# Loading the 1024-byte-piece weight tiles of a two-layer decoder kernel through two DMA queues

## The chip, the cores and the metric

The kernel runs on one core of one Trainium2 chip. The metric is the device time of one execution in microseconds (us); lower is better. Before the change the median of 3 runs is 270.51 us (270.24 to 270.66).

## The reference, cut to what matters

Two residual layers over 256 tokens of width 1024, all in float32. Each layer normalizes x, multiplies it with one wide input matrix, runs two attention groups on the columns, gates both and multiplies with an output matrix:

```python
for layer in range(DEPTH):                       # DEPTH = 2
    h = rmsnorm(x, norm_gain[layer])
    if layer % 2 == 0:
        proj = h @ w_in_ab[j]                    # 1024 x 4104
        qa, ka, va, ga, qb, kb_, vb_, gb, fb = split_cols(proj, AB_SIZES)
        ...                                      # MoBA attention ya, forgetting attention yb
        y = jnp.concatenate([ya * jax.nn.silu(ga), yb * jax.nn.silu(gb)], axis=-1)
        x = x + y @ w_out_ab[j]                  # 1024 x 1024
    else:
        proj = h @ w_in_cd[j]                    # 1024 x 3328
        qc, kc, vc, gc, qd, kd, vd, gd = split_cols(proj, CD_SIZES)
        ...                                      # differential attention yc, sliding-window attention yd
        y = jnp.concatenate([yc * jax.nn.silu(gc), yd * jax.nn.silu(gd)], axis=-1)
        x = x + y @ w_out_cd[j]
```

## The kernel before

All weights stream from HBM once, in 74 tiles of 512 KB. A tile is a list of parts (column offset, source slice), a number `nk` of 128-row blocks and a width. `wraws` (line 98) loads a tile into a float32 buffer `raw`: each of the 128 partitions receives `nk` rows of the matrix, so the DMA moves 128 x `nk` pieces of (width x 4) bytes. There are four `raw` buffers. `wload` (line 115) then splits the tile for float32-like accuracy: ScalarE (ACT) casts it to `whi` (line 123) and VectorE (DVE) subtracts, giving `wlo` (line 124). Five pairs of `whi`/`wlo` exist. TensorE (PE) multiplies three times per tile and row block (lines 261 to 263, or 430 and 432 for the gates).

Tiles come in three shapes: the first eight have pieces of 4096 bytes (`nk` = 1), most have pieces of 2048 bytes (`nk` = 2, 512 columns), and 22 have pieces of 1024 bytes (`nk` = 4, 256 columns). These 22, counted from 0 in the order of loading, are tiles 16 to 19 (the columns of `kb`, with 4 more columns copied in by GpSimd from `wf`, line 105), 24 to 31 (gates a and b), 52 and 53 (`kd` and `vd`), and 58 to 65 (gates c and d).

Every load is issued by the sync engine (SP) in tile order; SP waits at each for the `raw` buffer to come free, which is when DVE has made the `wlo` of the tile four places earlier. GpSimd (POOL) issues five small DMAs at the start (`params`, line 75, and `bcast`, line 81) and makes the four `wf` copies; after 43 us it has nothing to do.

The order of the work on PE is written out by hand (`tick`, line 149, steps through a list of units; generators such as `qk_heads`, line 342, `quad64`, line 528, and `scores`, line 477, are advanced between them). ACT and DVE run their instructions in the order in which they are issued there, so a cast that waits for its tile holds back what stands behind it. Around tiles 16 to 19 ACT's order is: cast of tile 16, `v`, `qf`, `qhi`, cast of tile 17, `kf` (line 392), first half of `khi` (line 399), cast of tile 18, second half of `khi`, cast of tile 19. On DVE the `wlo` of tile 18 stands ahead of the second half of `klo` (line 400), and `klo` ahead of the `wlo` of tile 19. PE needs `khi` and `klo` for the first attention scores (lines 490 and 494), which stand in its order behind tile 14's products and ahead of tile 15's.

Of the kernel before, what the change touches and what calls it, by code (L numbers as in the profile page):

```python
# [29 lines left out]
def trunk_kernel(  # L30
# [6 lines left out]
    nc = tc.nc  # L37
# [48 lines left out]
    last = {}  # L86
# [11 lines left out]
    def wraws(parts, nk, n, raw=None):  # L98
        if raw is None:
            raw = wraw.tile([128, WF], F32, name="raw")  # L100
        rv = raw[:, 0:nk * n].rearrange("p (k n) -> p k n", k=nk)
        for (c0, src) in parts:
            if isinstance(src, tuple):
                k0, f0 = src
                nc.gpsimd.tensor_copy(rv[:, :, c0:c0 + 4], wf[:, k0:k0 + nk, f0:f0 + 4])
                continue
            m = src.shape[1]
            last["sp"] = nc.sync.dma_start(rv[:, :, c0:c0 + m],
                                           src.rearrange("(k p) n -> p k n", p=128))
        k = len(wt) - KT  # L110
        if 0 <= k < KT:
            nc.sync.dma_start(wf[:, k, :], w_ab[k * 128:(k + 1) * 128, 4096:4104])
        return raw

    def wload(parts, nk, n, raw=None, pieces=1):
        if raw is None:
            raw = wraws(parts, nk, n)
        hi = wsp.tile([128, WF], F32R, name="whi")
        lo = wsp.tile([128, WF], F32R, name="wlo")
        m = nk * n // pieces  # L120
        for i in range(pieces):
            c = slice(i * m, (i + 1) * m)
            last["act"] = nc.scalar.copy(hi[:, c], raw[:, c])  # L123
            last["dve"] = nc.vector.tensor_tensor(out=lo[:, c], in0=raw[:, c], in1=hi[:, c].bitcast(F32),  # L124
                                    op=OP.subtract)
        return (hi[:, 0:nk * n].rearrange("p (k n) -> p k n", k=nk),
                lo[:, 0:nk * n].rearrange("p (k n) -> p k n", k=nk))
# [722 lines left out]
    with tc.manual_schedule():  # L850
        nc.vector.memset(wz, 0.0)
        raws = []
        for n in ("yth", "ytl"):
            r = act.tile([128, 2, 1024], F32, name=n)
            raws += [r[:, 0, :], r[:, 1, :]]
        xload(0)
        wraws(*tiles[0], raws[0])
        xload(1)
        for i in range(1, 4):
            wraws(*tiles[i], raws[i])  # L860
# [115 lines left out]
```

## Time and profile before

| what | value |
|---|---|
| median of 3 runs | 270.51 us (270.24 to 270.66) |
| the profiled execution's own time | 272.91 us |
| span of its profile, first to last instruction | 271.1 us |
| TensorE busy | 263.3 us, 97% of the span |
| mean granted TensorE clock | 0.994 |
| DMA, mean over the span | 153 GB/s |
| weight loads from `w_in_ab`, median issue to landing | 8.5 us |
| weight loads from `w_in_cd`, median issue to landing | 3.9 us |

Times inside the profile count from the first instruction. The own time of the profiled execution holds 1.81 us outside the span. A matmul's end is modelled: one of 512 columns is shown with some 0.39 us, while the next one starts 0.23 us after it, so back-to-back matmuls overlap in the rows and PE's idle time is only what is left between them. The granted clock is the share of full TensorE clock that the chip gave in a stretch.

### The profile page before, as it was taken

What the parts mean: (1) busy time and instruction counts of PE and PEld (TensorE: products, weight loads), DVE (VectorE), ACT (ScalarE), POOL (GpSimd) and SP (SyncE); (2) the same over time, 40 slices, a digit from 0 to 9 for tenths busy, and PEclk for the clock granted to TensorE, in tenths of its full rate; (3) what the DMA queues carried; (4) which work ended last, traced back from release to release, by engine and by line L of the source; (5) the groups of instructions that cost most, each with busy time, mean ns of one, the idle gap of its engine ahead of it and who ended that gap; (6) DMA issues with size and microseconds to landing.
All of it is one profiled execution on the core that took longest, in us unless ns stands there. A gap on an engine that the chain in (4) does not pass through costs nothing.

```text
span 271.1 us, 4378 instructions
## 1 busy us (share of the span) xinstructions
PE 263.3 (97%) x1535; PEld 216.7 (80%) x1535; DVE 213.1 (79%) x501; ACT 183.6 (68%) x411; POOL 6.3 (2%) x14
## 2 busy tenths in 40 slices
PE   7999999979999999999999999999999999999994
PEld 3787788769988688887788888888988789897884
DVE  5887895477997549997946988677898989899722
ACT  3788755676796757899726564457777999999300
POOL 4000040000000000000000000000000000000000
PEclk9999999979999999999999999999999999999999
DMA  6966964770363552814634668655418027207022
GB/s 247 336 196 166 302 182 112 263 221 3 98 182 105 149 167 58 251 27 143 210 104 166 175 183 290 201 160 167 146 34 274 6 77 232 81 8 224 2 77 77
DMA packets 27415, 41.36 MB, mean 153 GB/s; under 512 B 2801, under 2 KB 14466, under 8 KB 27394
## 3 DMA queue, kind: packets, MB, share of 16 engines
q1 hardware_dynamic: 27202, 41.07, 49.2%
q8 instruction: 12, 0.20, 0.3%
q14 instruction: 9, 0.07, 0.1%
q0 software_dynamic: 160, 0.01, 0.0%
q10 hardware_dynamic: 32, 0.01, 0.0%
HBM read 40.03 MB, written 1.05 MB: 152 GB/s over the span
## 4 chain that ended last, share of the span: by engine, by line
PE 74%; DMA 10%; DVE 8%; ACT 4%; issue 2%; SPq 1%; ACTq 0%
PE pj L261 16%; PE pj L263 16%; PE pj L262 16%; DMA raw<-in_w_in_ab_dram 9%; PE pj L430 8%; PE pj L432 4%; DVE wlo L124 3%; PE av L564 3%; PE at L522 3%; PE at L494 2%; PE at L382 2%; DMA wf<-in_w_in_ab_dram 1%; ACT e L505 1%; ACT e L503 1%; ACT whi L123 1%
## 5 line engine op out<-in xcount | busy, mean ns | idle before, releaser
L124 DVE TENSOR_TENSOR wlo<-raw,whi 128x1024 fp32r<-128x1024 f32 (+1 forms) x70 | 85.3, 1222 | 20.6 <-ACT whi L123 18.7
L123 ACT CAST whi<-raw 128x1024 fp32r<-128x1024 f32 (+1 forms) x70 | 72.8, 1048 | 31.0 <-PE pj L262 23.5
L261 PE MATMUL pj<-whi,hh 128*128 128x512 f32 (+2 forms) x192 | 72.8, 379 | 0.8 <-ACT whi L123 0.8
L263 PE MATMUL pj<-wlo,hh 128*128 128x512 f32 (+2 forms) x192 | 70.9, 369 | 0.2 <-DVE wlo L124 0.2
L262 PE MATMUL pj<-whi,hh 128*128 128x512 f32 (+2 forms) x192 | 70.8, 368 | 0.0
L430 PE MATMUL pj<-hh,whi 128*128 128x512 f32 x128 | 46.1, 401 | 0.2 <-DVE g L437 0.2
L261 PEld LDWEIGHTS pj<-whi,hh 128*128 128x128 f32 x192 | 36.5, 190 | 7.7 <-ACT whi L123 0.9
L263 PEld LDWEIGHTS pj<-wlo,hh 128*128 128x128 f32 x192 | 36.4, 189 | 7.5 <-DVE wlo L124 1.2
L262 PEld LDWEIGHTS pj<-whi,hh 128*128 128x128 f32 x192 | 36.4, 190 | 5.8 <-DVE hh L225 0.2
L432 PE MATMUL pj<-hh,wlo 128*128 128x256 f32 x128 | 35.8, 280 | 0.0
L430 PEld LDWEIGHTS pj<-hh,whi 128*128 128x128 f32 x128 | 24.1, 188 | 6.0 <-DVE g L437 0.4
L261 PE MATMUL pj<-whi,yth 128*128 128x512 f32 (+1 forms) x68 | 26.3, 387 | 0.0
L263 PE MATMUL pj<-wlo,yth 128*128 128x512 f32 (+1 forms) x68 | 25.9, 381 | 0.0
L262 PE MATMUL pj<-whi,ytl 128*128 128x512 f32 (+1 forms) x68 | 25.8, 380 | 0.0
L432 PEld LDWEIGHTS pj<-hh,wlo 128*128 128x128 f32 x128 | 24.2, 189 | 0.0
L503 ACT ACTIVATE e<-e,mn 128x128 f32<-128x128 f32 x32 | 12.5, 391 | 7.8 <-DVE mn L499 7.8
L505 ACT ACTIVATE e<-e,mn 128x256 f32<-128x256 f32 x32 | 15.9, 496 | 0.2 <-DVE mn L501 0.2
L261 PEld LDWEIGHTS pj<-whi,yth 128*128 128x128 f32 x68 | 12.8, 188 | 2.8 <-issue 0.3
L263 PEld LDWEIGHTS pj<-wlo,yth 128*128 128x128 f32 x68 | 12.8, 188 | 2.6
L262 PEld LDWEIGHTS pj<-whi,ytl 128*128 128x128 f32 x68 | 12.8, 188 | 2.5
L346 ACT ACTIVATE sq<-pj 128x512 f32<-128x512 f32 (+2 forms) x18 | 8.9, 509 | 4.3 <-PE pj L263 3.8
L347 DVE TENSOR_REDUCE qk_m<-sq 128x8 f32<-128x512 f32 (+2 forms) x18 | 10.1, 577 | 1.8 <-ACT sq L346 1.7
(159 smaller groups left out, 373.5 us busy)
## 6 DMA issues: line engine op xcount, KB each, us to landing
raw<-in_w_in_ab_dram SPq DMA_DIRECT2D x28, 512.0 KB, 8.5
raw<-in_w_in_cd_dram SPq DMA_DIRECT2D x26, 512.0 KB, 3.9
raw<-in_w_out_ab_dram SPq DMA_DIRECT2D x8, 512.0 KB, 5.3
raw<-in_w_out_cd_dram SPq DMA_DIRECT2D x8, 512.0 KB, 3.8
xs<-in_x_dram SPq DMA_DIRECT2D x2, 512.0 KB, 5.9
yth<-in_w_in_ab_dram SPq DMA_DIRECT2D x2, 512.0 KB, 6.8
ytl<-in_w_in_ab_dram SPq DMA_DIRECT2D x2, 512.0 KB, 7.7
out_dram<-xs SPq DMA_DIRECT2D x3, 256.0 KB, 2.0
```

Source lines behind the costliest of these rows:

```text
L123: last["act"] = nc.scalar.copy(hi[:, c], raw[:, c])
L124: last["dve"] = nc.vector.tensor_tensor(out=lo[:, c], in0=raw[:, c], in1=hi[:, c].bitcast(F32), op=OP.subtract)
L261: nc.tensor.matmul(ps, ah, bh, start=first, stop=False)
L262: nc.tensor.matmul(ps, al, bh, start=False, stop=False)
L263: nc.tensor.matmul(ps, ah, bl, start=False, stop=last)
L346: nc.scalar.activation(sq[:, 0:nh * HD], ps[t][:, 0:nh * HD], AF.Square)
L347: nc.vector.tensor_reduce(m[:, t, :], sq[:, 0:nh * HD].rearrange("p (h d) -> p h d", d=HD), axis=AX.X, op=OP.add)
L430: nc.tensor.matmul(pg, wh[:, i, w], hh[:, k].rearrange("p u t -> p (u t)"), start=k == 0, stop=False)
L432: nc.tensor.matmul(pg[:, 0:256], wl[:, i, w], hh[:, k, 0, :], start=False, stop=k == KT - 1)
L503: nc.scalar.activation(e[:, 0:128], e[:, 0:128], AF.Exp, bias=mn[:, 0:1], scale=-1.0, accum_out=sm[:, 0:1])
L505: nc.scalar.activation(e[:, 128:384], e[:, 128:384], AF.Exp, bias=mn[:, 1:2], scale=-1.0, accum_out=sm[:, 1:2])
L522: nc.tensor.transpose(pt[:, i * 128:(i + 1) * 128], blocks[j + i], ident)
```

## The change

In `wraws`, a part that is 256 columns wide is no longer loaded by one DMA of SP. GpSimd issues a DMA for the second half of its row blocks (two of four), and SP one for the first half. All other loads stay as they were. The consumer of a tile now waits for both.

```diff
             m = src.shape[1]
-            last["sp"] = nc.sync.dma_start(rv[:, :, c0:c0 + m],
-                                           src.rearrange("(k p) n -> p k n", p=128))
+            sv = src.rearrange("(k p) n -> p k n", p=128)
+            if m == 256:
+
+                nc.gpsimd.dma_start(rv[:, nk // 2:nk, c0:c0 + m], sv[:, nk // 2:nk, :])
+                last["sp"] = nc.sync.dma_start(rv[:, 0:nk // 2, c0:c0 + m], sv[:, 0:nk // 2, :])
+                continue
+            last["sp"] = nc.sync.dma_start(rv[:, :, c0:c0 + m], sv)
```

The order of instructions on PE, DVE and ACT is the same before and after. On GpSimd, before the change, the four copies of tiles 16 to 19 (`raw_601`, `raw_659`, `raw_687`, `raw_727`) stand right behind the small DMAs of the start:

```order
L75 DMA prow_88<-in_moba_k_gain_dram 1x2x64
L75 DMA prow_88<-in_fox_q_gain_dram 1x2x64
L75 DMA prow_88<-in_fox_k_gain_dram 1x2x64
L81 DMA bfor_303<-in_b_forget_dram 128x8
L105 COPY raw_601<-wf_89 128x4x4
L105 COPY raw_659<-wf_89 128x4x4
L105 COPY raw_687<-wf_89 128x4x4
L105 COPY raw_727<-wf_89 128x4x4
```

After it, each copy stands behind the DMA of its tile's second half, and 18 more such DMAs follow (tiles 24 to 31, 52, 53 and 58 to 65):

```order
L75 DMA prow_88<-in_fox_k_gain_dram 1x2x64
L81 DMA bfor_303<-in_b_forget_dram 128x8
L111 DMA raw_601<-in_w_in_ab_dram 128x2x256
L105 COPY raw_601<-wf_89 128x4x4
L111 DMA raw_660<-in_w_in_ab_dram 128x2x256
L105 COPY raw_660<-wf_89 128x4x4
L111 DMA raw_689<-in_w_in_ab_dram 128x2x256
L105 COPY raw_689<-wf_89 128x4x4
L111 DMA raw_730<-in_w_in_ab_dram 128x2x256
L105 COPY raw_730<-wf_89 128x4x4
L111 DMA raw_1045<-in_w_in_ab_dram 128x2x256
```

The copies have moved behind one DMA issue each; nothing else of GpSimd's has moved. On ACT, around tiles 16 to 18, the casts wait after the change for a DMA of each kind (DMAHW is SP's, DMASW is GpSimd's; the line numbers are five higher than before):

```order
L414 ACTIVATE v_530<-pj_427,n_r_334 128x512 [waits PE_49]
L128 CAST whi_605<-raw_601 128x1040 [waits DMASW5_49,DVE_49,DMAHW3_49,PE_49,Pool_49]
L414 ACTIVATE v_530<-pj_428,n_r_334 128x512 [waits PE_49]
L397 ACTIVATE qf_107<-at_533,pcol_90 128x512 [waits PE_49]
L404 ACTIVATE qhi_108<-at_539,pcol_90 128x512 [waits PE_49]
L128 CAST whi_664<-raw_660 128x1040 [waits DMASW6_49,DVE_49,DMAHW4_49,PE_49,Pool_49]
L397 ACTIVATE kf_110<-at_567,pcol_90 128x512 [waits PE_49]
L404 ACTIVATE khi_111<-at_567,pcol_90 128x4x128
L128 CAST whi_693<-raw_689 128x1040 [waits DVE_49,DMASW7_49,PE_49,DMAHW5_49,Activation_49,Pool_49]
```

Before the change the same casts stood at the same places and waited for SP's DMA alone; what moved is only which DMAs they wait for.

## Rows read from the trace of the kernel before

**Rows 1.** The page: span, and the first row of the engines' busy time.
```profile
span 271.1 us, 4378 instructions
...
PE 263.3 (97%) x1535; PEld 216.7 (80%) x1535; DVE 213.1 (79%) x501; ACT 183.6 (68%) x411; POOL 6.3 (2%) x14
```

**Rows 2.** The chain that ended last, 40 to 62 us: start us, us, what.
```profile
40.24 12.79 DMA raw<-in_w_in_ab_dram
...
53.13 1.06 ACT whi L123
...
55.38 0.76 DVE klo L400
...
56.18 0.39 PE at L494 x2
...
57.43 0.72 PE pj L261
...
60.48 0.23 PE pj L262
...
61.64 0.12 PE pj L261
```

**Rows 3.** Timeline of PE, the first scores (53 us) and the second (71 us).
```profile
53.63 0.49 PE L490 MATMUL at<-kf,qf 64*128 64x128 f32 x4
...
57.36 0.79 PE L261 MATMUL pj<-whi,hh 128*128 128x512 f32 x1
...
71.51 0.49 PE L490 MATMUL at<-kf,qf 64*128 64x128 f32 x4
...
72.07 0.28 PE L494 MATMUL at<-klo,qhi 64*128 64x256 f32 x2
...
72.87 0.39 PE L261 MATMUL pj<-whi,hh 128*128 128x260 f32 x1
```

**Rows 4.** Windows: stretch us, PE, PEld, DVE, ACT, POOL busy (x), PEclk, DMA share, GB/s.
```profile
41.00:46.50 5.50, 5.50 (x30) 4.59 (x29) 2.92 (x5) 2.13 (x3) 0.20 (x1) 1.00 0.38 107
49.00:51.50 2.50, 2.50 (x15) 2.04 (x14) 0.88 (x2) 1.62 (x3) 0.00 (x0) 1.00 0.88 306
...
57.40:60.20 2.80, 2.80 (x9) 2.22 (x8) 2.09 (x16) 2.69 (x13) 0.00 (x0) 0.52 0.85 267
...
184.25:185.50 1.25, 1.25 (x7) 1.03 (x6) 1.25 (x2) 0.60 (x1) 0.00 (x0) 1.00 0.99 345
```

**Rows 5.** Timeline of ACT: the cast of tile 17, and `khi` behind it.
```profile
49.88 1.06 ACT L123 CAST whi<-raw 128x1040 fp32r<-128x1040 f32 x1 [1.31 <-DMA raw<-in_w_in_ab_dram]
...
51.43 0.68 ACT L399 ACTIVATE khi<-at,pcol 128x512 fp32r<-128x512 f32 x1
```

**Rows 6.** Line 108: the loads issued 37.5 to 43.5, then those 67 to 77 us.
```profile
DMA to landing us min/median/max: 8.1/10.8/12.8
...
DMA to landing us min/median/max: 7.0/8.5/9.6
```

**Rows 7.** POOL: two of its DMAs (KB, us to landing), one's issue, and copies.
```profile
prow<-in_moba_q_gain_dram POOLq DMA_DIRECT2D x1, 0.5 KB, 6.0
...
bfor<-in_b_forget_dram POOLq DMA_DIRECT2D x1, 4.0 KB, 5.0
...
4.23 0.57 POOL L81 DMA_DIRECT2D bfor<-in_b_forget_dram  x1
37.64 2.83 POOL L105 COPY raw<-wf 128x16 f32<-128x16 f32 x3 [32.83 <-DMA raw<-in_w_in_ab_dram]
```

**Rows 8.** Later loads: tile 24's cast; gates c and d, loads and first casts.
```profile
76.98 1.03 ACT L123 CAST whi<-raw 128x1024 fp32r<-128x1024 f32 x1
...
L108 SPq DMA_DIRECT2D raw<-in_w_in_cd_dram x8: 367/368/368, 182.4 to 206.1; - x8
...
L123 ACT CAST whi<-raw x4: 1043/1048/1053, 196.3 to 203.8; 128x1024 fp32r<-128x1024 f32 x4
```

**Rows 9.** Timeline of PE, the layer-1 scores that wait for `khi`.
```profile
212.25 0.39 PE L494 MATMUL at<-khi,qhi 64*128 64x256 f32 x2 [0.23 <-ACT khi L399]
```

## The prediction

> **What bounds the kernel now.** I read the page first [rows 1]: TensorE (PE) is busy for 263.3 of 271.1 us. A kernel in that state gains only where PE stands still or runs slowly, so the next view is the chain that ended last [rows 2]. Over most of the span it runs through PE itself. The reader should see the one place after the start where it leaves PE for a transfer: a weight load from `w_in_ab` issued at 40.24 us takes 12.79 us, lands at 53.03, and is followed by a cast on ACT (53.13), `klo` on DVE (55.38) and the scores on PE (56.18). That load is the third 1024-byte-piece tile, tile 18.
>
> The timeline of PE gives the price of this place [rows 3]. The first scores start at 53.63 and the next product at 57.36, 3.73 us later. The same scores for the other half start at 71.51 and are over at 72.87, 1.36 us. So 2.37 us are lost in them. PE then does tile 15's twelve products of 512 columns from 57.43 to 61.64, 4.21 us [rows 2]; at 60.48 one takes 0.23, and twelve would take 2.80, so another 1.41 us are lost. The window view tells why [rows 4]: from 57.4 to 60.2 the granted clock is 0.52 of full speed, about the lower of its two levels (1.2 of 2.4 GHz), after PE had stood and waited; in the other windows shown it is 1.00. **In all 3.78 us hang on late `khi` and `klo`.**
>
> Then the transfers themselves. The four loads issued from 37.6 to 43.0 us take 8.1 to 12.8 us to land [rows 6]. While they are under way, from 41 to 46.5, the DMA engines are busy for 0.38 of the time and move 107 GB/s [rows 4], although two to three loads wait in SP's queue. That is what a second queue could use.
>
> **The change, part by part.** *What must be gained for the stall to go.* At the second scores `klo` is used 0.56 us after the first score matmul starts (71.51 to 72.07) [rows 3], so the first scores want it at 53.63 + 0.56 = 54.19. From tile 18's landing to that use the chain takes 56.18 - 53.03 = 3.15 us [rows 2]. Tile 18 must land by 51.04, 2.0 us earlier. Its cast also stands behind the first part of `khi`, and that behind tile 17's cast, which started at 49.88 when its load came [rows 5]. `khi` ends near 52.1, and tile 18's cast would have to start at 51.14, so tile 17 has to land about 1 us earlier too. The three loads 16 to 18 are 1.57 MB in 15.4 us, from 37.6 to 53.03, or 102 GB/s; 13.4 us would do, 117 GB/s. **A rate 15% higher removes the whole stall.**
>
> *The transfer with two queues.* No row shows a large load on GpSimd's queue, so I bound it. From below: both queues move 107 GB/s, 214 together, and tile 18 is there 1.57 MB / 214 GB/s = 7.3 us plus a start of some 2 us after 37.6, near 47; the stall is gone with much to spare. From above: the total stays at 107 GB/s [rows 4], GpSimd's queue gets half of it, and it starts only after the 6.0 us that the slowest of its small DMAs takes from issue to landing [rows 7]. Its three halves, 0.79 MB at 53.5 GB/s, take 14.7 us, and tile 18 lands at 37.6 + 6.0 + 14.7 = 58.3, 5.3 us later than now. I take a rate well over 117 GB/s, because the nearest row is the stretch itself, where the engines are idle for 0.62 of the time, and because pieces of this size run at 306 GB/s (49 to 51.5 us) and 345 GB/s (184.25 to 185.5) elsewhere [rows 4]. The Trainium skill ("DMA: Bandwidth & Descriptors", section "Latency and other measured facts") gives about 1 us to the first byte for a DMA of GpSimd; with it in place of 6.0 the upper end would be an estimated 53.3. No row here shows such a load by itself, and the small DMAs took 5.0 and 6.0 us to land under full engines [rows 7].
>
> *Issues.* SP's 22 issues stay, at 0.37 us each [rows 8], and halve in size: nothing. GpSimd gets 22 more. The broadcast to 128 partitions took it 0.57 us [rows 7], the nearest row; 22 x 0.57 = 12.5 us on an engine busy for 6.3 us of the span [rows 1], whose only other work there is the four copies of line 105. Three copies take 2.83 us from 37.64 [rows 7]. Behind the DMAs tile 18's half is issued after two DMAs and two copies, 2 x (0.57 + 0.94) = 3.0 us after 37.6, so near 40.7, 0.4 us after SP's half at 40.24. The copy of tile 16 ends near 37.6 + 0.57 + 0.94 = 39.1, far ahead of its load's landing at 37.6 + 8.1 = 45.7 [rows 6]. Cover for all of it: the transfer. Cost: nothing.
>
> *New waits.* Each of the 22 casts now waits for the later half; behind a waiting cast on ACT stand `kf` and `khi`, and behind its `wlo` on DVE stands `klo`: that is the chain above, and no other engine's order changes. *Later tiles.* Tile 24 is issued at 67.5 and lands 7.0 us later (74.5) [rows 6], and is cast at 76.98 [rows 8]: 2.5 us to spare. The first load of gates c is issued at 182.4 and cast at 196.3 [rows 8]. The 18 tiles after the first four therefore bring nothing when faster and cost nothing up to 2.5 us of delay.
>
> *Sum.* 272.91 us is the profiled execution's own time. From it go 3.78 us. I give back 0.23, because in layer 1, where no load is late, the same scores still wait 0.23 us for `khi` [rows 9]: 272.91 - 3.55 = 269.36. That execution is 2.40 us above the median of the runs shown, so the forecast for the median is 270.51 - 3.55 = **267.0 us**.
>
> **The rivals.** *No gain.* The limit may lie behind the queues, in the memory or in how the rows of `w_in_ab` fall in it. For it: in 41 to 46.5 the rate stays at 107 GB/s with loads queued, while the very same queue and piece size reach 306 and 345 GB/s [rows 4], so the queue is not always what limits. Against it: the engines stand idle meanwhile, and two halves take their rows from different places at a time. Then tile 18 lands near 53.03 as before and the time is 270.5. The Trainium skill speaks for this rival and against the change ("DMA: Bandwidth & Descriptors", section "Issuing engines are not separate DMA queues"): DMAs of all issuers run on the same 16 engines and interleave, and a second issuer saves only issue time. By it alone the 3.55 us would be 0. The trace agrees that issuing is short; it cannot show two bulk queues.
>
> *A part of it.* The rate rises by less than 15%, tile 18 lands 0.5 to 2 us earlier, and the wait shrinks by as much; each us of landing is worth a us of waiting and some of the low clock: 268 to 270.
>
> *Slower: the half on GpSimd's queue comes last.* Place: the casts of tiles 17 and 18. It decides once GpSimd's half of tile 18 lands after 53.03. From there each us costs PE one us, since khi, klo and scores follow it directly. For it: the small DMAs' 5.0 to 6.0 us [rows 7], and the queue's order, in which each DMA stands behind the copy of the tile before. Against it: the issue is only 0.4 us later, and a late start leaves SP's halves the engines alone, so they finish early. With 2 us of lateness: 270.51 + 2.0 = 272.5; at the upper end above, 5.3 us, 275.8. That the change does nothing it says is excluded: the order of instructions shows 22 new DMAs on GpSimd and the halved ones on SP.
>
> **How the numbers follow.** Stall gone: 0.45. A part of it: 0.13. No gain: 0.19. Slower: 0.23. A difference of under 0.2% (0.54 us) can't be told from none; the three runs spread by 0.42. So faster 0.58, same 0.19, slower 0.23. The likeliest case has its own range of 266.5 (all 3.78 us, 266.7, and the runs' spread) to 268.0. The range starts at 266.5, takes in the partial case and no gain (to 270.9), and the milder part of the slower case, 1 us, to 271.6; what is left out is the rest of the slower case.
>
> **What would show it.** Right: the four loads from 37.6 us land in clearly less than 8.1 to 12.8 us, windows from 41 to 46.5 show far more than 107 GB/s, ACT's casts of tiles 16 to 18 no longer wait for a DMA, the first scores take near 1.4 us, and the granted clock stays at 1.00 through tile 15's products. Wrong: 107 GB/s again in that stretch (no gain), or casts that wait for GpSimd's DMA beyond 53 us (slower). My step fails also if the stall goes and the end does not move by it, so that ACT or DVE were just behind.

## The result and the profile after

| | before | after |
|---|---|---|
| median of the first runs | 270.38 us (4 runs, 270.13 to 270.66) | 273.89 us (4 runs, 273.12 to 276.28) |
| ratio to before, 95% interval | | 1.0123 [1.0093, 1.0154] |
| once more, on another chip | 271.15 us (30 runs) | 273.12 us (12 runs), 1.0062 [1.0036, 1.0088] |
| profiled execution | 272.91 us, span 271.1 | 274.57 us, span 272.8 |

The change makes the kernel slower, by 0.6 to 1.2%. The prediction was 267.0 us, faster.

The page of the changed kernel first: PE is as busy as before, GpSimd has 20.0 us of work instead of 6.3, and two slices of the clock's row are below 9, where one was.

```profile
span 272.8 us, 4477 instructions
...
PE 264.4 (97%) x1535; PEld 217.8 (80%) x1535; DVE 213.5 (78%) x501; ACT 183.5 (67%) x411; POOL 20.0 (7%) x36
...
PEclk9999999968999999999999999999999999999999
...
q1 hardware_dynamic: 21570, 35.30, 41.6%
q0 software_dynamic: 1920, 5.78, 8.9%
```

The windows of the changed kernel (columns as in [rows 4]). The stretch that the second queue was to fill moves 105 GB/s, where it moved 107. The DMA engines' busy share went from 0.38 to 0.60 for it: more busy, no more bytes.

```profile
41.00:46.50 5.50, 5.50 (x29) 4.59 (x28) 2.81 (x5) 2.09 (x3) 1.23 (x4) 1.00 0.60 105
...
58.10:63.30 5.20, 5.20 (x14) 4.11 (x15) 3.15 (x15) 3.79 (x18) 0.00 (x0) 0.55 0.48 150
```

The landings of tile 18's two halves, by the line that issues them (SP is line 112 now, GpSimd 111). The whole tile landed 12.8 us after its issue at 40.24 [rows 2, 6]. Now SP's half lands 13.2 us after 40.13, at 53.30, and GpSimd's 12.0 us after 40.40, at 52.41.

```profile
L112 SPq DMA_DIRECT2D raw<-in_w_in_ab_dram x1: 367/367/367, 40.1 to 40.1; - x1
...
DMA to landing us min/median/max: 13.2/13.2/13.2
...
L111 POOL DMA_DIRECT2D raw<-in_w_in_ab_dram x1: 712/712/712, 40.4 to 40.4; - x1
...
DMA to landing us min/median/max: 12.0/12.0/12.0
```

The timeline of PE at the first scores, to be read beside [rows 3]. The two waits, for `khi` and `klo`, are 1.09 and 0.85 us.

```profile
53.52 0.49 PE L495 MATMUL at<-kf,qf 64*128 64x128 f32 x4
55.09 0.39 PE L499 MATMUL at<-khi,qhi 64*128 64x256 f32 x2 [1.09 <-ACT khi L404]
...
56.45 0.58 PE L499 MATMUL at<-klo,qhi 64*128 64x256 f32 x2 [0.85 <-DVE klo L405]
...
58.03 0.79 PE L266 MATMUL pj<-whi,hh 128*128 128x512 f32 x1
```

The same two waits in the kernel before, 0.71 and 0.84 us:

```profile
54.83 0.39 PE L494 MATMUL at<-khi,qhi 64*128 64x256 f32 x2 [0.71 <-ACT khi L399]
...
56.18 0.39 PE L494 MATMUL at<-klo,qhi 64*128 64x256 f32 x2 [0.84 <-DVE klo L400]
```

And the chain that ended last, beside [rows 2].

```profile
42.92 11.06 DMA raw<-in_w_in_ab_dram
...
54.36 0.69 ACT khi L404
...
55.65 0.76 DVE klo L405
...
56.45 0.58 PE at L499 x2
...
58.10 0.72 PE pj L266
...
62.23 0.43 PE pj L266
62.66 0.36 PE pj L267
63.02 0.23 PE pj L268
63.26 0.12 PE pj L266
```

The view follows ACT's wait back to tile 19's load (issued at 42.92). But `khi` stands ahead of the cast of tile 19 and behind that of tile 18, and ACT's timeline shows it starting 0.96 us after the latter:

```profile
53.40 1.06 ACT L128 CAST whi<-raw 128x1040 fp32r<-128x1040 f32 x1 [1.29 <-PE pj L267]
54.36 0.68 ACT L404 ACTIVATE khi<-at,pcol 128x512 fp32r<-128x512 f32 x1
```

The cast starts 0.10 us after SP's half lands at 53.30, as it started 0.10 us after the whole tile landed at 53.03 in the kernel before. The row names PE as what it waited for; in the profiles below where tile 18 lands by 47.7 us the same cast starts at 50.1 to 50.5, so PE does not hold it as long as that.

What the reader is to see: the same steps as before, a little later at each. `klo` starts at 55.65 instead of 55.38 (+0.27), tile 15's products at 58.10 instead of 57.43 (+0.67), the first product of 260 columns at 63.26 instead of 61.64 (+1.62). That is nearly all of the 1.7 us between the spans. Only 0.27 us of it is the later `klo`. The rest is the clock: 0.50 granted from 56.0 to 58.1 and 0.55 from 58.1 to 63.3, so that ten of the twelve products take 0.43 us or more.

**The runs lie in two groups.** Each run lists the granted clock of its span. The kernel before was run 138 times beside the experiments: 112 runs at a clock of 0.997 or more lie from 270.2 to 272.2 us, median 271.0, and 26 runs at 0.994 or less from 272.6 to 274.5, median 273.0. The low clock costs 2.0 us, and comes in 26 of 138 runs. In each of the five profiles taken in such a run (of before, the change, `q1_kb_whole_gpsimd`, `p1_second_pair_far` and `p3_rows_interleaved`) the clock is below 1.00 between 56 and 63 us, right behind the late scores; in the other fifteen it is 1.00 there. Of the change's 16 runs only 4 are at 1.00 (271.7 to 272.1, median 271.85), 12 are lower (272.9 to 276.3). So the change costs 0.85 us at full clock, and takes the kernel from 19% to 75% of runs with the low clock (on one chip side by side, 4 of 30 and 8 of 12). Below, runs are counted by these groups: "low" means 0.994 or less. (The ratios leave out two runs of `e1_kb_only`, one of `r2_gpsimd_halves_16_to_18` and one of before as disturbed, 274.5 to 276.4 us; the counts keep them.)

### The profile page after: what moved, and what is told of

It is laid out like the page before. It is cut to its first block, busy times and chain, and to the rows that moved or that the text cites. A ratio compares the mean times of both kernels' runs of the same rounds, so it can differ in the third digit from the quotient of the medians.

```text
span 272.8 us, 4477 instructions
## 1 busy us (share of the span) xinstructions
PE 264.4 (97%) x1535; PEld 217.8 (80%) x1535; DVE 213.5 (78%) x501; ACT 183.5 (67%) x411; POOL 20.0 (7%) x36
## 4 chain that ended last, share of the span: by engine, by line
PE 77%; DMA 9%; DVE 5%; ACT 4%; issue 1%; SPq 1%; DVEq 0%; ACTq 0%
PE pj L266 18%; PE pj L267 17%; PE pj L268 17%; PE pj L435 8%; DMA raw<-in_w_in_ab_dram 8%; PE pj L437 4%; PE av L569 3%; PE at L527 3%; DVE wlo L129 3%; PE at L499 2%; PE at L387 2%; DMA wf<-in_w_in_ab_dram 2%; ACT e L510 1%; ACT e L508 1%; ACT whi L128 1%
## 5 line engine op out<-in xcount | busy, mean ns | idle before, releaser
L111 POOL DMA_DIRECT2D raw<-in_w_in_cd_dram x10 | 7.1, 710 | 108.3 <-DVE wlo L129 91.8
L266 PEld LDWEIGHTS pj<-whi,yth 128*128 128x128 f32 x68 | 12.8, 188 | 2.8 <-issue 0.3
L268 PEld LDWEIGHTS pj<-wlo,yth 128*128 128x128 f32 x68 | 12.8, 188 | 2.6
L267 PEld LDWEIGHTS pj<-whi,ytl 128*128 128x128 f32 x68 | 12.8, 188 | 2.5
L111 POOL DMA_DIRECT2D raw<-in_w_in_ab_dram x12 | 8.5, 712 | 79.0 <-DVE rs_r2x L188 33.1
```

Of the source, the lines that this page charges most:

```text
L111: nc.gpsimd.dma_start(rv[:, nk // 2:nk, c0:c0 + m], sv[:, nk // 2:nk, :])
L266: nc.tensor.matmul(ps, ah, bh, start=first, stop=False)
L267: nc.tensor.matmul(ps, al, bh, start=False, stop=False)
L268: nc.tensor.matmul(ps, ah, bl, start=False, stop=last)
```

## The experiments

In all of them PE's instructions stand in the order of the kernel before. Where lines were added, blank ones were taken out above, so lines differ by a few.

### Which tiles, and is it the cutting?

Theory K: the loss is made at the `kb` tiles. L: at the 18 later tiles. S: by cutting a load in two.

`e1_kb_only`: two queues only where a tile has a gate column copied in, that is for `kb`.

```diff
-            if m == 256:
+            if m == 256 and len(parts) == 2:
```

> Two queues for the four kb tiles 16 to 19 alone; the other 18 tiles are loaded by SP whole, as before. Theory K (the loss comes from the kb place: the rate from 41 to 46.5 us stays near 107 GB/s, a half of tile 18 lands some 0.3 us later than the whole did, and the low clock after it lasts longer): all of the loss is here, 273 to 275 us. Theory L (the loss comes from the 18 later tiles, whose casts wait for a late half or whose GpSimd work disturbs others): as before, 270.4. Theory S (cutting a load in two costs, whatever queue carries the halves): 273 to 275 here as under K, so this run does not tell K from S; the run with both halves on SP does.

Measured: 272.0 us median, ratio 1.0017 [0.9979, 1.0055], 4 of 12 runs low; at full clock 271.78, 0.8 above before's 271.00 of the same session. The loss is here, but in the median less than K's 273 to 275. SP's half of tile 18 lands 13.4 us after issue.

`e2_rest_only`: the other 18 tiles.

```diff
-            if m == 256:
+            if m == 256 and len(parts) == 1:
```

> Two queues for the 18 tiles of the gates and kd/vd alone; the four kb tiles are loaded by SP whole, as before. K: 270.2 to 270.9, like the kernel before. L: 272.5 to 275, most or all of the loss of 3.5 us.

Measured: 270.94 us, ratio 0.9977 [0.9951, 1.0003], none of 12 low. L falls: the later tiles cost nothing.

`e3_sp_halves`: both halves on SP, for all 22 tiles.

```diff
-                nc.gpsimd.dma_start(rv[:, nk // 2:nk, c0:c0 + m], sv[:, nk // 2:nk, :])
-                last["sp"] = nc.sync.dma_start(rv[:, 0:nk // 2, c0:c0 + m], sv[:, 0:nk // 2, :])
+                nc.sync.dma_start(rv[:, 0:nk // 2, c0:c0 + m], sv[:, 0:nk // 2, :])
+                last["sp"] = nc.sync.dma_start(rv[:, nk // 2:nk, c0:c0 + m], sv[:, nk // 2:nk, :])
```

> All 22 tiles in two halves as in the change, both issued by SP, first rows first; no second queue. If the second queue is what costs (K's form of it): 270.2 to 271.0, since SP's issues of 0.37 us lie beside transfers of several us and the rows come in the same order as before. Theory S: 273 to 275, as the change. Tile 18 lands at 53.0 us under the first, at 53.3 or later under S.

Measured: 270.69 us, 0.9976 [0.9949, 1.0003], none of 12 low; tile 18's later half lands at 52.30. S falls. What costs is the second queue, at four tiles.

### Is the rate the queue's, and what is the stall worth?

`e4_kb_from_cd`: the kernel before with the `kb` tiles from the other matrix.

```diff
-        proj(w_ab, 2560 + 256 * j, 256, post_kb(j), extra=4 * j)
+        proj(w_cd, 1536 + 256 * j, 256, post_kb(j), extra=4 * j)
```

> The kernel before, one queue, but the kb tiles take their 1024-byte pieces from w_in_cd (columns 1536 to 2047) instead of w_in_ab; kb is thus computed from other weights. Theory M (the rate of 107 GB/s belongs to the addresses: these pieces in w_in_ab): the four loads land 3.7 to 6 us after issue, the first scores no longer wait, the clock stays at 1.00, and the time is 270.4 - 3.55 = 266.9 (266.5 to 267.5). If one queue or the piece size sets the rate: they land 8 to 13 us after issue as before, and the time is 270.4. Either way this shows what the whole stall is worth, which the prediction put at 3.55 us.

Measured: 269.29 us, 0.9931 [0.9907, 0.9954], 11 runs within 0.28 us, none low. The window of this run:

```profile
41.00:46.50 5.50, 5.50 (x29) 4.59 (x29) 4.37 (x7) 4.34 (x6) 0.20 (x1) 1.00 0.92 293
```

One queue, the same piece size, 293 GB/s instead of 107. Tiles 16 to 18 land 4.8 to 5.8 us after issue, and the scores no longer wait, as its timeline of PE shows:

```profile
53.79 0.49 PE L490 MATMUL at<-kf,qf 64*128 64x128 f32 x4
54.03 0.37 PE L494 MATMUL at<-khi,qhi 64*128 64x256 f32 x2
...
54.35 0.28 PE L494 MATMUL at<-klo,qhi 64*128 64x256 f32 x2
```

So theory M holds on the rate, but its price was wrong: with no stall the kernel takes 269.3, not 266.9.

`c1_change_kb_from_cd`: the same edit in the changed kernel, two queues.

> The change with its two queues for all 22 tiles, but the kb tiles from w_in_cd (kb is computed from other weights). Theory M (the limit is in the addresses of w_in_ab, whatever queue): these tiles land 4 to 7 us after issue as with one queue, and the time is 269.2 to 269.8, no better and no worse than 269.3. If GpSimd's queue is itself slow (its packets 0.49 us each in the slow stretch): its halves land 8 us or more after issue here too, and the time is 270.5 or more.

Measured: 269.25 us, 0.9922 [0.9893, 0.9951], none of 7 low; halves land 4.1 to 5.7 us after issue. With these addresses the second queue neither helps nor harms.

### Does the loss run through `khi`?

Theory K2: the change makes the wait a little longer, and the low clock, which then comes more often, is the larger part. K1: a fixed delay.

`a1_change_again` is the change itself.

> The change itself once more, beside the others on one chip, with more runs. Theory K2 (the change makes the wait of the first scores some 0.3 to 0.5 us longer, and what costs more is that PE then more often falls to the lower clock, 2 to 5 us each time): the runs lie in groups, near 271 us at clock 1.00 and at 273 to 276 where the granted clock of the span is 0.984 to 0.994, the second group more frequent than in the kernel before (10 of 34); median 272.0 to 273.9. Theory K1 (a fixed delay of some 3 us, the same in every run): all runs within 273 to 275.

Measured: 273.12 us, 8 of 12 low; 271.67 to 272.07 at full clock. K2's two groups, not K1's single one. The profiled run is at full clock: SP's half of tile 18 lands 13.6 us after issue, the waits are 1.48 and 0.85 us, and the first product of 260 columns starts at 60.59. In the profile above it is 63.10 on the same view, though the waits are shorter: there the clock fell.

```profile
55.48 0.39 PE L499 MATMUL at<-khi,qhi 64*128 64x256 f32 x2 [1.48 <-ACT khi L404]
...
56.83 0.39 PE L499 MATMUL at<-klo,qhi 64*128 64x256 f32 x2 [0.85 <-DVE klo L405]
...
60.59 0.28 PE L266 MATMUL pj<-whi,hh 128*128 128x260 f32 x1
```

`h1_before_khi_first`: the kernel before, with the cast of tile 18 behind the second `khi` on ACT, and its subtraction behind the second `klo` on DVE. (`kk` holds the last `khi` and `klo` instruction; `held` puts tile 18 off by one tick, until they are traced.)

```diff
+            es = behind(kk) if len(wt) == 18 else ExitStack()
+            with es:
...
+            if len(wt) == 18 and not at.setdefault("held", 0):
+                at["held"] = 1
+                return
             wt.append(wload(*tiles[len(wt)]))
```

> The kernel before, one queue, but the cast of tile 18 on ACT stands behind the second khi, and its subtraction on DVE behind the second klo, so that the first scores no longer hang on tile 18. K2: the waits of 0.71 and 0.84 us and the low clock go, whatever the transfer does: 269.0 to 269.7, as with the kb tiles from w_in_cd (269.3), and all runs at clock 1.00. If tile 18 is needed by something else soon after: 270 or more, with a new wait at the products of tile 18.

Measured: 270.0 us, 0.9952 [0.9932, 0.9973], none of 12 low. The rate is the old one (109 GB/s) and tile 18 lands 12.1 us after issue, but the first scores no longer wait for it. The median is 0.3 us above K2's 269.0 to 269.7. The profile has no wait of PE at tile 18's products, and no run here shows what the 0.3 us are. Its timeline of ACT, both `khi` now in one row ahead of the cast:

```profile
49.84 1.07 ACT L123 CAST whi<-raw 128x1040 fp32r<-128x1040 f32 x1 [1.23 <-DMA raw<-in_w_in_ab_dram]
50.81 0.68 ACT L392 ACTIVATE kf<-at,pcol 128x512 f32<-128x512 f32 x1
51.39 1.26 ACT L399 ACTIVATE khi<-at,pcol 128x512 fp32r<-128x512 f32 x2
52.54 1.06 ACT L123 CAST whi<-raw 128x1040 fp32r<-128x1040 f32 x1
```

`h2_change_khi_first`: the same order in the changed kernel.

> The change, with the same order of cast and khi as in the run before it. K2: the late halves of tile 18 cost nothing now, 269.0 to 269.9, clock 1.00. If GpSimd's transfers cost in another way as well (other casts late, DVE slowed by GpSimd's work): above that run by what they cost, 270.5 to 273.

Measured: 270.37 us, 0.9971 [0.9941, 1.0001], 1 of 12 low; 270.24 at full clock, where the change has 271.85. SP's half of tile 18 still lands late (12.9 us after issue), and most of the loss is gone: against `h1_before_khi_first` the change costs 0.24 us at full clock in place of 0.85. So the loss runs through the cast that stands ahead of `khi`, as K2 has it. The median lies between the two forecasts (269.9 and 270.5); the profile has one new wait of PE, 0.47 us at 64.62, later in the attention.

`h3_before_khi_first_17_18`: as `h1_before_khi_first`, with tile 17 as well (`len(wt) in (17, 18)`).

> The kernel before, one queue, with the casts of both tile 17 and tile 18 behind the second khi (and their subtractions behind the second klo), so that nothing before the first scores hangs on the slow loads; the scheduler puts some later casts elsewhere too. If the spread of the run with tile 18 alone (269.2 to 271.1) comes from tile 17's landing: 269.2 to 269.8 with a spread under 0.5. If something else makes that spread, or the moved casts cost: 270.0 or more.

Measured: 269.92 us, 0.9957 [0.9936, 0.9977], none of 12 low, from 269.3 to 270.9. No narrower than with tile 18 alone, so tile 17's landing does not make that spread. Moving its cast too has a price: the profile has a new wait of PE, 0.65 us at 67.45. `h1_before_khi_first` and this one beat both kernels, by 0.4 to 0.5% against before.

### Why is tile 18 later with two queues?

`q1_kb_whole_gpsimd`: the four `kb` tiles whole on GpSimd's queue.

```diff
+            kb = m == 256 and len(parts) == 2
+            d = (nc.gpsimd if kb else nc.sync).dma_start(rv[:, :, c0:c0 + m], src.rearrange("(k p) n -> p k n", p=128))
...
```

> The four kb tiles whole on GpSimd's queue, nothing of them on SP's; the other tiles on SP as before. If what makes tile 18 late in the change is that two queues share one limited rate, so that halves of tiles 18 and 19 are under way together: here one queue serves the tiles one after the other, tile 18 lands at 52.0 to 53.1 us as before, 271.0 (270.5 to 271.6). If GpSimd's queue itself is slower: tile 18 lands after 53.4, 272 or more.

Measured: 272.68 us, 1.0049 [1.0016, 1.0081], 7 of 12 low; tile 18 lands at 53.76. GpSimd's queue alone is the slower one: from 46.5 to 49 us this run moves 131 GB/s, the kernel before 188. First this run, then before:

```profile
46.50:49.00 2.50, 2.50 (x14) 2.07 (x13) 1.49 (x2) 2.22 (x4) 0.00 (x0) 1.00 0.80 131
...
46.50:49.00 2.50, 2.50 (x15) 2.06 (x14) 1.64 (x2) 2.08 (x4) 0.00 (x0) 1.00 0.63 188
```

`r2_gpsimd_halves_16_to_18`: GpSimd's halves for tiles 16 to 18 alone (`and len(wt) < 19` added to the condition of `e1_kb_only`).

> Two queues for tiles 16 to 18 alone; tile 19 whole on SP, behind SP's half of tile 18. If the later landing of tile 18 with two queues comes from tile 19's half, which GpSimd's queue carries while SP's half of tile 18 is still under way: tile 18 now lands by 52.9 us, as with one queue or sooner, and the time is 270.5 to 271.2. If GpSimd's queue or its 4096-byte packets delay SP's pieces: 53.3 us or later, 271.7 or more.

Measured: 271.32 us, 1.0001 [0.9972, 1.0030], 3 of 12 low. Tile 18's later half lands at 53.06, between the two forecasts: tile 19's half is a part of it at most, and two profiles of the change itself lie further apart (53.30 and 53.68).

`r3_act_queue_halves`: the second halves of the four `kb` tiles on ScalarE's hardware queue.

```diff
-                nc.gpsimd.dma_start(rv[:, nk // 2:nk, c0:c0 + m], sv[:, nk // 2:nk, :])
+                nc.scalar.dma_start(rv[:, nk // 2:nk, c0:c0 + m], sv[:, nk // 2:nk, :])
```

> The second half of the four kb tiles on ScalarE's hardware queue in place of GpSimd's software queue; the scheduler also moves ACT's cast of tile 16 behind qhi, and the issues cost ACT 0.4 us each or more, so the landings count here, not the time. If it is GpSimd's queue that makes tile 18 late: its later half lands at 52.0 to 53.0 us, like one queue. If any second queue does: 53.3 us or later. The rate from 41 to 46.5 us is 107 GB/s under both. Time 270.5 to 272.

Measured: 271.02 us, 0.9984 [0.9965, 1.0002], none of 12 low. Tile 18's halves land at 51.48 and 52.25, as early as with one queue. So it is GpSimd's queue, not a second queue as such. The queues' rows for the window from 41 to 46.5 us (packets, MB, share of 16 engines) show this side by side. First the kernel before:

```profile
q1 hardware_dynamic: 588, 0.59, 38.2%
```

The change:

```profile
q0 software_dynamic: 80, 0.26, 39.5%
q1 hardware_dynamic: 327, 0.32, 20.1%
```

`q1_kb_whole_gpsimd`:

```profile
q0 software_dynamic: 160, 0.59, 82.8%
```

`r3_act_queue_halves`:

```profile
q10 hardware_dynamic: 305, 0.30, 19.9%
q1 hardware_dynamic: 311, 0.30, 18.9%
```

Four ways of issuing, 0.58 to 0.60 MB each. And here a byte on GpSimd's queue, in 4096-byte packets, keeps an engine busy about twice as long (82.8% against 38.2% for 0.59 MB). That goes with these addresses: in `c1_change_kb_from_cd` the two queues, in the same window, take about the same.

```profile
q0 software_dynamic: 258, 0.83, 43.8%
q1 hardware_dynamic: 802, 0.77, 42.5%
```

How the longer busy time makes tile 18 late is not shown. That it does go with GpSimd's queue rests on all the profiles together, since one kernel's landing differs by some tenths of a us and more from run to run (the same four loads land tile 18 at 53.03 in before and at 52.01 in `e2_rest_only`). With the original addresses tile 18 landed at 52.0 to 53.03 in the six profiles with hardware queues alone (before, `e2_rest_only`, `e3_sp_halves`, `h1_before_khi_first`, `h3_before_khi_first_17_18`, `r3_act_queue_halves`), and at 53.06 to 53.76 in the six with GpSimd's.

### What makes these pieces slow?

All six are the kernel before with one queue and other addresses for `kb`.

`p1_second_pair_far`: tiles 18 and 19 from columns far from those of 16 and 17, `(2560, 3584)[j]` in place of `2560 + 256 * j`.

> The kernel before, one queue, but tiles 18 and 19 take columns 3584 to 3839 of w_in_ab in place of 2816 to 3071, which lie beside the columns of tiles 16 and 17 (kb's second half is computed from other weights). Theory A (pieces whose rows were just read beside them come at over 200 GB/s, first ones at 107): now tiles 18 and 19 are first ones too, tile 18 lands near 54.7 (49.8 + 0.52 MB / 107 GB/s) and tile 19 near 59.6, and the time is 272.5 to 275. Theory O (it does not matter which columns, only that the first two loads of a group are slow): tile 18 lands at 52 to 53, as before, 271.

Measured: 274.69 us, 1.0131 [1.0101, 1.0160], all 4 runs low. ACT's casts of tiles 18 and 19:

```profile
53.89 1.06 ACT L123 CAST whi<-raw 128x1040 fp32r<-128x1040 f32 x1 [2.17 <-DMA raw<-in_w_in_ab_dram]
...
59.47 1.06 ACT L123 CAST whi<-raw 128x1040 fp32r<-128x1040 f32 x1 [3.93 <-DMA raw<-in_w_in_ab_dram]
```

In the kernel before these casts start at 53.13 and 54.68. Tile 19 comes as theory A has it (59.6), tile 18 between A's 54.7 and theory O's 52 to 53. So the second pair is quick in the kernel before most likely because its pieces lie beside the first pair's. That is not shown: no run loads the second pair's columns ahead of the first pair's. Nor is it enough, since the first pair lies beside the columns of `qb`, loaded just before as tiles 12 to 15, and is slow all the same.

`p3_rows_interleaved`: partition p takes rows 4p to 4p+3, `"(p k) n -> p k n"`.

> The kernel before, one queue, same columns and same 1024-byte pieces of w_in_ab, but partition p of a kb tile takes rows 4p to 4p+3 of its 512 instead of rows p, 128+p, 256+p and 384+p, so that the pieces that are under way at one time lie elsewhere in memory (kb is computed with rows in the wrong order). If the 107 GB/s come from which rows are read together: tiles 16 to 18 land 4 to 7 us after issue, the first scores do not wait, 269.3. If any 1024-byte pieces of these columns are slow: 8 to 12.8 us, 271.

Measured: 273.11 us, 1.0047 [1.0020, 1.0075], 7 of 12 low; 107 GB/s again, 8.2 to 13.3 us. The order of the rows is not it. The time is above the 271 that was forecast for this case: tile 18 lands at 53.56 here, with SP's queue alone.

`r1_cd_shifted_32B`: `e4_kb_from_cd` from column 1544 on.

> The kernel before, one queue, kb tiles from w_in_cd as in the earlier run that landed them 4.8 to 5.8 us after issue, but from columns 1544 on, 32 bytes further, so that no piece starts at a multiple of 1024 bytes, as in w_in_ab, whose rows are 16416 bytes long (kb is computed from other weights). If the start of the pieces makes the 107 GB/s: 8 us and more for the first two loads, 107 GB/s from 41 to 46.5 us, 271. If the distance between rows makes it: 4.8 to 6 us, over 250 GB/s, 269.3.

Measured: 269.37 us, 0.9933 [0.9909, 0.9958], 309 GB/s. A start 32 bytes off is not it.

`r4_kb_from_wo_ab`: `proj(wo_ab, 256 * j, ...)`.

> The kernel before, one queue, kb tiles from w_out_ab (columns 0 to 511; rows 4096 bytes apart, pieces at multiples of 1024 bytes; kb is computed from other weights). If row distances near a multiple of 4096 bytes make the slow rate: 8 us and more after issue, 107 GB/s from 41 to 46.5 us, 271. If only pieces that start off a multiple of 1024 bytes are slow: 4.8 to 6 us after issue, 269.3.

Measured: 269.30 us, 0.9924 [0.9894, 0.9954], 313 GB/s. A row distance of 4096 bytes is not it.

`s1_ab_rows_17440B` and `s2_cd_rows_16416B`: pieces at a distance set by hand, here the first.

```diff
+            if extra is not None:
+                parts = [(0, bass.AP(tensor=w_ab.tensor, offset=w_ab.offset + j // 4 * 1969920 + c0, ap=[[4360, 512], [1, 256]]))]
```

> The kernel before, one queue, 1024-byte pieces of w_in_ab, but for the kb tiles the next piece lies 17440 bytes further in place of 16416 (a diagonal through the matrix; some of its bytes have been read before; kb is computed from other weights). If the distance of 16416 bytes makes the slow rate: 5 to 6 us after issue, over 250 GB/s from 41 to 46.5 us, 269.3. If the matrix or its place makes it: 8 us and more, 107 GB/s, 271.

Measured: 269.28 us, 0.9935 [0.9910, 0.9960]. The window:

```profile
41.00:46.50 5.50, 5.50 (x30) 4.59 (x29) 4.38 (x7) 4.10 (x6) 0.20 (x1) 1.00 0.92 294
```

> The converse: kb pieces from w_in_cd, which landed 4.8 to 5.8 us after issue with rows 13312 bytes apart, now 16416 bytes apart, as in w_in_ab (kb is computed from other weights). If the distance makes the slow rate: first loads 8 us and more after issue, 107 GB/s from 41 to 46.5 us, 271. If the matrix makes it: 4.8 to 6 us, over 250 GB/s, 269.3.

Measured: 269.26 us, 0.9927 [0.9901, 0.9952]. The window:

```profile
41.00:46.50 5.50, 5.50 (x29) 4.59 (x29) 4.21 (x7) 4.09 (x6) 0.20 (x1) 1.00 0.97 252
```

`w_in_ab` at another distance is quick (some of those bytes had been read before). `w_in_cd` at the distance of 16416 bytes is slower than at its own (252 against 293 GB/s; tiles land 5.9 to 7.6 us after issue instead of 4.8 to 5.8), but far from 107. So the distance seems to have a part in it (the two runs also read other bytes of the matrix) and is not all of it. What else belongs to it stays open.

## Why the prediction was wrong

- **The step that failed:** "I take a rate well over 117 GB/s". The rate stayed at 105. The argument was that idle DMA engines (0.38 busy) and waiting loads leave room for a second queue. But what held the loads back goes with the addresses and not with the queue: with GpSimd, with ScalarE's queue, or with GpSimd alone the engines moved 0.58 to 0.60 MB in the same 5.5 us, and with other addresses one queue moved 293 GB/s. The text had both readings and the row that decided (the very same queue and piece size at 345 GB/s in [rows 4]); it weighed the idle engines higher. The trace of the kernel before also held a second such stretch: with the first gate tiles of the same matrix, from 69 to 77 us, the engines were busy for 0.38 of the time and moved 112 GB/s. The rule of the Trainium skill that it quoted against the change ("DMA: Bandwidth & Descriptors", section "Issuing engines are not separate DMA queues") agrees with these rows.
- **The rival that came true** is "slower", at the place and from the point named: the cast of tile 18, once a half lands after 53.03. It is SP's half that comes last (53.30), not GpSimd's, which is issued 0.27 us later and lands 0.89 earlier. The price named, one us for each us of lateness, left out the clock: in the profiled execution 0.27 us of lateness came with a lower clock for longer, 1.62 us in all. At full clock the price holds: from `e2_rest_only`, whose `kb` loads are those of the kernel before, to `a1_change_again` tile 18 lands 1.67 us later (52.01 and 53.68) and the profiled execution is 1.70 us longer (270.37 and 272.07). Over the runs the change costs 0.85 us at full clock, and the low clock's 2.0 us in 75% of runs instead of 19%.
- **The sum was also mis-sized.** Its first half, 272.91 - 3.55 = 269.36 for the profiled execution, is what the kernels without the stall take: 269.25 to 269.37 in six kernels with other addresses. Its second half, taking the same 3.55 us from the median of the runs, was wrong. The profiled execution lay 2.40 us above the median because it is one of those with the low clock, and the median is not. From the median the whole stall is worth 271.0 - 269.3 = 1.7 us. Had the rate risen, the result would have been 269.3, outside the likeliest case's own range.
- **What was right:** the stall hangs on late `khi` and `klo` behind tile 18 (`h1_before_khi_first` removes it with the transfer unchanged); the issues cost nothing, though GpSimd's took 0.71 us each and not 0.57; the 18 later tiles cost nothing (`e2_rest_only`).

## What to carry to other kernels

Idle DMA engines with loads queued do not show that a queue is short: look in the same trace for the same queue and piece size at a higher rate elsewhere, and if it is there, ask about the addresses first. Where a load can't be made faster, look at what stands behind its first reader on each engine: here one cast put behind `khi` gave 0.5% with the same loads at the same rate. And ahead of a sum, ask whether the profiled execution is a typical one: a clock that fell in it is in the sum, but need not be in the median.

## What was not expected of the hardware

- From 41 to 46.5 us, 1024-byte pieces of `w_in_ab`, 16416 bytes apart, come at 104 to 111 GB/s on every queue; pieces of the same size from `w_in_cd`, from `w_out_ab`, or on a diagonal through `w_in_ab` at 292 to 313. The second pair of tiles is quicker: the window from 49 to 51.5 us moves 306 GB/s [rows 4], about a fifth of it already in pieces of 2048 bytes, which the prediction took for pieces of 1024. Taken from other columns the pair lands later (`p1_second_pair_far`). The Trainium skill ("DMA: Bandwidth & Descriptors", section "Latency and other measured facts") reports rates that fall, down to about half, for rows at large powers of two apart, from 512 KiB to 8 MiB in its list, and offers as a guess that the streams meet in the same memory channels. 16416 bytes is 32 more than 16 KiB. `s2_cd_rows_16416B` agrees in its sign only, 252 for 293 GB/s; the 107 of `w_in_ab` is not explained by it.
- With the slow addresses a byte on GpSimd's queue kept the DMA engines busy about twice as long as one on SP's at the same rate, and tile 18 landed later; with those of `w_in_cd` it took about as long.
- The low clock comes in some runs of a kernel and not in others. The profiled run of `a1_change_again` waited 1.48 and 0.85 us and stayed at 1.00; the profiled run of the kernel before waited less, 0.71 and 0.84, and fell. In the kernels that keep tile 18's cast ahead of the second `khi` and whose tile 18 landed by 52.3 us in the profile (`e2_rest_only`, `e3_sp_halves`, `r3_act_queue_halves`) none of 36 runs was low, nor any of 24 where the cast stood behind `khi` with SP's queue alone. Each kernel's landing is that of one profile, and the `kb` loads of `e2_rest_only` are those of the kernel before, which was low in 10 of 34 runs beside it. What decides it in a single run, these traces do not show.
